# Stores of late projections issued from the ACT queue instead of the SP queue, in a one-core hybrid attention and S5 layer

## The chip, the cores and the metric

The kernel runs on one core of a Trainium2 chip. The metric is the time of one execution in microseconds of device time; for the kernel before, the median of three runs is 1052.14 us. The profile is of one execution whose own time is 1050.65 us and whose span from the first to the last instruction is 1048.8 us.

The engines are named as in the profile: PE (TensorE) multiplies matrices, DVE (VectorE), ACT (ScalarE) and POOL (GpSimd) work on elements, and SP (SyncE) does nothing but issue DMAs. ACT can issue DMAs too, between its other instructions. Each engine takes its instructions strictly in the order in which they stand in its queue, and an instruction that waits for a semaphore holds up everything behind it.

## The reference

One layer of a streaming encoder, for 1024 prompt tokens and 64 sample tokens (1088 columns in all), width 1024, in float32:

```python
h = rms_norm(x, g_norm) * (1.0 + scale[:, None, :]) + shift[:, None, :]
z = h @ w_in
zq, zk, zv, zqi, zki, zwi, zga, zu, zgs, zma, zmb = split_cols(z)
...
o_attn = dsa_attend(q, qi, wi, pos, k_all, v_all, ki_all, kpos, n_sel)
branch_a = (o_attn * jax.nn.silu(zga)) @ w_attn_proj
y_ssm, h_re, h_im = s5_mix(zu, h0, lambda_re, lambda_im, log_dt, ssm_b_re, ssm_b_im,
                           ssm_c_re, ssm_c_im, d_skip)
g_lin = jax.nn.gelu(y_ssm).astype(x.dtype) @ w_glu
y_glu = g_lin[..., :SSM_WIDTH] * jax.nn.sigmoid(g_lin[..., SSM_WIDTH:])
branch_b = (y_glu.astype(x.dtype) * jax.nn.silu(zgs)) @ w_ssm_proj
merged = jax.nn.sigmoid(zma) * branch_a + jax.nn.sigmoid(zmb) * branch_b
x = x + gate[:, None, :] * (merged @ w_out)
```

`dsa_attend` selects the best keys for each query by an indexer's scores and attends to them; `s5_mix` is a complex linear recurrence over the tokens.

## The kernel before, in words

Every product of float32 matrices is made of three products of parts: `hhi` and `hlo` are the normalized input, split into a high and a low part, `whi` and `wlo` the parts of a block of 128 columns of weights. L201 and L202 multiply `whi` with both parts of h, L206 `wlo` with the high one. A block of weights comes in two halves: for each, `load_split` has SP load `raw` (L163, 256 KB), ACT cast it to `whi` (L156) and POOL make the rest `wlo` (L157). The tiles `raw`, `whi` and `wlo` have two buffers each. The tokens are cut into three chunks of 384, 384 and 320 columns; a chunk of a block takes 8 matmuls of each of the three lines.

The projections q, u (zu), ma (zma), mb (zmb), the gate of attention (zga) and the gate of the S5 branch (zgs) are called late products here. One generator, `products(jobs)`, makes them block by block, and the program takes a few steps from it wherever another stage leaves PE free. So late products are woven into the index stage, the attention and the S5 stage, until about 800 us. Each chunk ends in an `evac`: ACT copies the result out of PSUM (`us` in `proj_u`, L604; `st` in `proj_store`, L611) or applies Silu (`sg` in `gate_s`, L627), and the chunk is stored to a tensor in HBM (`u_d`, L605; `q_d`, `ma_d` or `mb_d`, L612; `gs_d`, L628). These stores, 88 in all, are issued by SP.

The order within each engine's queue is the work of a scheduler, which orders what the program records by priorities and its own idea of times. `tc.issue_after(ins)` is a scheduling hint about what is recorded under it.

Around 720 to 770 us the S5 stage makes its outputs for blocks of groups, q = 0 to 3. SP loads the tables `tq` (L1342) and `cs` (L1347), then stores the outputs of the block before, eight stores `y_d<-yb` (L1447), stores `kp_d` (L1338), and loads the states `zq` (four loads of 136 KB, L1434). PE then computes with L1442 (`tq`) and L1443 (`zq` with `cs`), ACT copies the result to `yb` (L1444). Between them stand late products of `gate_s`. Later, four gelus on ACT (L1494, L1495), a split on DVE (L1496, L1497) and the GLU's products (L201, tiles `big`) follow.

In the built program each DMA that SP or ACT issues gets one of eight semaphores, DMAHW0 to DMAHW7, in turn; the order in which the scheduler records the DMAs of both queues decides whose turn it is. A DMA that takes a semaphore waits, in its engine's queue, until the DMA before it on that semaphore has landed.

Of the kernel before, what the change touches and what calls it, by code (L numbers as in the profile page):

```python
# [33 lines left out]
P = 128  # L34
# [23 lines left out]
BO = (7, 3, 4, 5, 6, 2, 1, 0, 8)  # L58
# [25 lines left out]
def hybrid_step(ctx, tc, ins, outs):  # L84
    nc = tc.nc
    act, dve, pool, pe, sync = nc.scalar, nc.vector, nc.gpsimd, nc.tensor, nc.sync
# [31 lines left out]
    def tmp(name="tmp"):  # L118
        return tmpp.tile([P, 384], F32, tag="tmp", name=name)

    q_d = dram.tile([4, P, TOK], F32, name="q_d")
    u_d = dram.tile([512, 8, NCH], F32, name="u_d")
# [3 lines left out]
    gs_d = dram.tile([4, P, TOK], F32, name="gs_d")  # L126
# [64 lines left out]
    last_mm = [None]  # L191
# [403 lines left out]
    stored = [None]  # L595

    def proj_u(m):
        def evac(c, t0, n, ps):
            s = tmp("us")
            npr = min(n, 1024 - t0)  # L600
            for o, w, n0 in ((0, npr, 8 + t0 // 8), (npr, n - npr, 0)):
                if w:
                    part = s[:, o:o + w].rearrange("p (s n) -> p s n", s=8)
                    act.copy(part, ps[:, o:o + w].rearrange("p (n s) -> p s n", s=8))  # L604
                    stored[0] = sync.dma_start(u_d[m * P:(m + 1) * P, :, n0:n0 + w // 8], part)  # L605
        return w_in, C_U + m * P, evac

    def proj_store(dst, c0, m):
        def evac(c, t0, n, ps):
            s = tmp("st")  # L610
            act.copy(s[:, :n], ps[:, :n])  # L611
            stored[0] = sync.dma_start(dst[m, :, t0:t0 + n], s[:, :n])  # L612
        return w_in, c0 + m * P, evac

    def gate_a(m):
# [7 lines left out]
    def gate_s(m):  # L623

        def evac(c, t0, n, ps):
            s = tmp("sg")
            act.activation(s[:, :n], ps[:, :n], AF.Silu)  # L627
            sync.dma_start(gs_d[m, :, t0:t0 + n], s[:, :n])  # L628
        return w_in, C_GS + m * P, evac

    jobs = [proj_store(q_d, C_Q, m) for m in range(4)] + [proj_u(m) for m in range(4)]
# [586 lines left out]
    ready = next(first)  # L1218
# [5 lines left out]
    def heads():  # L1224
        nonlocal ready
        pt = tokp.tile([P, 2, 2, 4, 2, P], F32R, tag="wtok", name="pt")
        keys, vals = kst, [vst]
        other = None
        for i, b in enumerate(BO):
            if b == 8:  # L1230
                ck = atq.tile([P, 4, P], F32, tag="qt", name="ck", bufs=1)
                sync.dma_start(ck, ins["cache_k"][0, 0].rearrange("(a p) g d -> p a (g d)", p=P))
                keys = rb.tile([P, 2, 2, 576], F32R, tag="t2", name="kss")
                build_keys(keys, None, [(ck[:, i], P) for i in range(4)] + [(ktok[:64, 8], 64)])
            st, mx = ready
            for h in range(8):
                other = Head(b, h, st, mx, keys, vals, pt, other)
                yield other
                if h == QH and b < 8:
                    ready = list(att_queries(BO[i + 1]))[1]  # L1240
                if h == VH and b == 8:
                    cv = atq.tile([P, 4, 2, 64], F32, tag="qt", name="cv", bufs=1)
                    sync.dma_start(cv, ins["cache_v"][0, 0].rearrange("(a p) g d -> p a g d", p=P))
                    vals.append(kvp.tile([P, 5, 2, 2, 64], F32R, tag="v", name="vss"))
                    split(vals[1][:, 0:4, :, 0, :], vals[1][:, 0:4, :, 1, :], cv)
                    split(vals[1][:64, 4, :, 0, :], vals[1][:64, 4, :, 1, :], vnew)
        for _ in range(3):
            yield None
# [179 lines left out]
    def ssm_out(q):  # L1428
        cs, tq = ca_t[q], tq_t[q]
        rs = slice(4 * q, 4 * q + 4)  # L1430
        zq = ssp.tile([P, 4, 2, NCH], F32, tag="eq", name="zq")
        for j in range(2):
            for g2 in range(2):
                sync.dma_start(zq[64 * j:64 * j + 64, :, g2, :], z4[64 * g2:64 * g2 + 64, j, rs, 0:NCH])  # L1434
        yield
        yb = ssp.tile([P, 8, NCH], F32, tag="yb", name="yb")
        for g0, ng in ((0, 3), (3, 3), (6, 2)):
            ps = bank1()
            for i in range(ng):
                g = g0 + i  # L1440
                o = ps[:, i * NCH:(i + 1) * NCH]
                pe.matmul(o, tq[:, g, :], uall[:, 8 * q + g, :], start=True, stop=False)  # L1442
                pe.matmul(o, cs[:, g // 2, g % 2, :], zq[:, g // 2, g % 2, :], start=False, stop=True)  # L1443
            act.copy(yb[:, g0:g0 + ng, :], ps[:, :ng * NCH].rearrange("p (g n) -> p g n", n=NCH))  # L1444
        yv = y_d[P * q:P * q + P].rearrange("(g c) t n -> c g t n", c=16)
        for t in range(8):
            sync.dma_start(yv[:, :, t, :], yb[16 * t:16 * t + 16])  # L1447
# [80 lines left out]
    for m in range(4):  # L1528
        w, nxt = nxt, load_pair(*pairs[m + 1])
        for t0, n in CH:  # L1530
            gs, s = two_tmps("gs", "sg")
# [34 lines left out]
    for m in range(8):  # L1566
        w = nxt
# [38 lines left out]
    for h in range(2):  # L1606
# [6 lines left out]
        for t in range(9):  # L1613
            t0, nt = tok_tile(t)
# [19 lines left out]
            dst = outs["y_prompt"][0, t0:t0 + nt] if t < NT else outs["y_sample"][0]  # L1634
# [61 lines left out]
```

## Time and profile before

| | |
|---|---|
| median of three runs (lowest, highest) | 1052.14 us (1051.26, 1052.95) |
| the profiled execution: own time, span | 1050.65 us, 1048.8 us |
| PE busy, share of the span | 978.5 us, 93% |
| DVE busy | 661.5 us, 63% |
| ACT busy | 459.0 us, 44% |
| POOL busy | 296.0 us, 28% |
| PE's longest waits | 11.56 us at 658.8 us, 9.52 us at 277.3 us, 5.05 us at 269.3 us |

The two waits near 270 and 277 us are for `whi` casts behind the selection of keys, the one at 658.8 us for an ACT instruction that stands behind a cast. In the attention, 300 to 545 us, PE is busy for 243.15 of 245 us. The granted clock of PE is full nearly everywhere and half for some microseconds after each of these long waits.

### The profile page before, as it was taken

What the parts mean: (1) busy time and instruction counts of PE and PEld (TensorE: products, weight loads), DVE (VectorE), ACT (ScalarE), POOL (GpSimd) and SP (SyncE); (2) the same over time, 40 slices, a digit from 0 to 9 for tenths busy, and PEclk for the clock granted to TensorE, in tenths of its full rate; (3) what the DMA queues carried; (4) which work ended last, traced back from release to release, by engine and by line L of the source; (5) the groups of instructions that cost most, each with busy time, mean ns of one, the idle gap of its engine ahead of it and who ended that gap; (6) DMA issues with size and microseconds to landing.
All of it is one profiled execution on the core that took longest, in us unless ns stands there. A gap on an engine that the chain in (4) does not pass through costs nothing.

```text
span 1048.8 us, 16634 instructions
## 1 busy us (share of the span) xinstructions
PE 978.5 (93%) x5948; PEld 887.9 (85%) x5948; DVE 661.5 (63%) x1400; ACT 459.0 (44%) x975; POOL 296.0 (28%) x438
## 2 busy tenths in 40 slices
PE   7777999999499999999998999599999999999997
PEld 1476887998389999999888999598999999998786
DVE  6774898899557777868647699900016556654244
ACT  3575567321167666666633321112273344442122
POOL 3475202531352211222117264454124000001200
PEclk9898999999699999999999999799999999999999
DMA  8730301153342211222248331344764354535133
GB/s 300 230 93 21 90 1 48 43 165 132 71 98 49 62 46 40 59 59 74 70 94 127 98 91 49 84 101 102 191 172 130 93 169 148 166 105 162 55 132 116
DMA packets 141765, 108.41 MB, mean 103 GB/s; under 512 B 32894, under 2 KB 128680, under 8 KB 141680
## 3 DMA queue, kind: packets, MB, share of 16 engines
q1 hardware_dynamic: 140160, 105.05, 36.1%
q10 hardware_dynamic: 1232, 2.23, 0.6%
q8 instruction: 47, 0.77, 0.3%
q14 instruction: 38, 0.31, 0.1%
q0 software_dynamic: 288, 0.05, 0.0%
HBM read 77.79 MB, written 25.17 MB: 98 GB/s over the span
## 4 chain that ended last, share of the span: by engine, by line
PE 61%; DVE 20%; ACT 5%; POOL 4%; issue 4%; DMA 3%; SPq 1%; POOLq 0%; DVEq 0%; ACTq 0%
PE acc L201 12%; PE acc L206 12%; PE acc L202 12%; PE o L1083 3%; PE big L201 3%; PE big L202 3%; PE big L206 3%; PE sc L1040 3%; PE tp L1066 3%; DVE gt L908 2%; DMA raw<-in_w_in 2%; DVE sc L706 2%; DVE near_v L915 1%; DVE t L1381 1%; POOL hlo L559 1%
## 5 line engine op out<-in xcount | busy, mean ns | idle before, releaser
L201 PE MATMUL acc<-hhi,whi 128*128 128x384 f32 (+1 forms) x768 | 257.2, 339 | 26.2 <-ACT whi L156 14.6
L202 PE MATMUL acc<-hlo,whi 128*128 128x384 f32 (+1 forms) x768 | 252.1, 333 | 0.0
L201 PEld LDWEIGHTS acc<-hhi,whi 128*128 128x128 f32 x768 | 146.5, 191 | 31.8 <-ACT whi L156 16.3
L157 POOL TENSOR_TENSOR wlo<-raw,whi 128x512 fp32r<-128x512 f32 x64 | 88.4, 1395 | 293.9 <-ACT whi L156 159.8
L206 PE MATMUL acc<-hhi,wlo 128*128 128x384 f32 (+1 forms) x768 | 150.1, 334 | 0.0
L202 PEld LDWEIGHTS acc<-hlo,whi 128*128 128x128 f32 x768 | 146.6, 191 | 0.6
L206 PEld LDWEIGHTS acc<-hhi,wlo 128*128 128x128 f32 x768 | 129.7, 190 | 1.9 <-POOL gw L1167 0.9
L156 ACT CAST whi<-raw 128x512 fp32r<-128x512 f32 x64 | 38.0, 620 | 72.3 <-DMA raw<-in_w_in 55.0
L1496 DVE CAST ghi<-gt 128x1088 fp32r<-128x1088 f32 x4 | 3.2, 808 | 103.1 <-DMA raw<-in_w_in 100.0
L1071 DVE TENSOR_TENSOR pt<-tp,pt 128x512 fp32r<-128x512 f32 (+3 forms) x112 | 57.0, 518 | 17.7 <-ACT pt L1070 16.8
L611 ACT COPY st<-acc 128x384 f32<-128x384 f32 (+1 forms) x60 | 27.9, 465 | 89.5 <-PE acc L206 86.7
L1050 ACT ACTIVATE pm<-pm,mx 128x1024 f32<-128x1024 f32 (+8 forms) x72 | 56.1, 779 | 24.7 <-DVE mx L1043 24.2
L1070 ACT CAST pt<-tp 128x512 fp32r<-128x512 f32 (+3 forms) x112 | 49.3, 450 | 35.9 <-PE tp L1066 34.6
L1631 POOL TENSOR_TENSOR yh<-yh,gfin 128x512 f32<-128x512 f32 (+1 forms) x9 | 11.6, 1292 | 173.3 <-ACT xr L1627 173.3
L1043 DVE CUSTOM_DVE_ANT_0 pm<-sc,bias 128x512 f32<-128x512 f32 (+4 forms) x72 | 42.6, 593 | 26.8 <-PE sc L1040 26.2
L201 PE MATMUL acc<-wohi,mhi 128*128 128x512 f32 (+2 forms) x152 | 56.7, 377 | 0.0
L202 PE MATMUL acc<-wolo,mhi 128*128 128x512 f32 (+2 forms) x152 | 56.7, 377 | 0.0
L1066 PE MATMUL tp<-ident,pm 128*128 128x128 f32 (+2 forms) x328 | 52.8, 270 | 0.7 <-DVE pt L1071 0.5
L1040 PE MATMUL sc<-kst,qs 128*128 128x512 f32 (+3 forms) x192 | 51.8, 352 | 0.1
L1083 PE MATMUL o<-pt,vst 128*128 128x256 f32 x288 | 47.6, 292 | 1.0 <-DVE pt L1071 0.9
L1066 PEld LDWEIGHTS tp<-ident,pm 128*128 128x128 f32 (+2 forms) x328 | 38.5, 139 | 9.7 <-DVE pt L1071 2.3
L706 DVE SCALAR_TENSOR_TENSOR sc<-relu,wi,sc 128x512 f32<-128x512 f32 (+5 forms) x42 | 42.8, 1020 | 3.8 <-ACT relu L704 1.0
(484 smaller groups left out, 2244.0 us busy)
## 6 DMA issues: line engine op xcount, KB each, us to landing
raw<-in_w_in SPq DMA_DIRECT2D x68, 256.0 KB
wm<-in_w_mod SPq DMA_DIRECT2D x16, 512.0 KB
xt<-in_x_prompt SPq DMA_DIRECT2D x8, 512.0 KB
gw<-in_w_mod SPq DMA_DIRECT2D x2, 2048.0 KB
raw<-in_w_out SPq DMA_DIRECT2D x16, 256.0 KB
xr<-in_x_prompt SPq DMA_DIRECT2D x16, 256.0 KB
ma_d<-st SPq DMA_DIRECT2D x16, 192.0 KB
mb_d<-st SPq DMA_DIRECT2D x16, 192.0 KB
```

The lines of the kernel that those rows point to most:

```text
L157: rest_on[0].tensor_tensor(lo, raw, hi.bitcast(F32), op=OP.subtract)
L201: pe.matmul(ps, lhi(k), rhi(k), start=(k == 0), stop=False)
L202: pe.matmul(ps, lhi(k), rlo(k), start=False, stop=False)
L206: last_mm[0] = pe.matmul(ps, llo(k), rhi(k), start=False, stop=(k == nk - 1))
L706: dve.scalar_tensor_tensor(scores[b][:nq], r[:nq, :n], w, scores[b][:nq], op0=OP.mult, op1=OP.add, accum_out=sums[:nq, 0, col] if h == 4 e ...
L1040: pe.matmul(ps, self.st[:, self.h // 2, self.h % 2, :nq], self.keys[:, self.h // 4, j, c:c + m], start=(j == 0), stop=(j == 1))
L1043: dve.tensor_tensor_reduce(out=self.pm[:, c:c + m], in0=ps, in1=bias[self.b][:nq, c:c + m], op0=OP.add, op1=OP.min, scale=-0.125, scalar=t ...
L1050: act.activation(self.pm, self.pm, AF.Exp, bias=self.ng, scale=-1.0, accum_out=self.sm)
L1066: pe.transpose(tp[:rows, i, :nq], self.pm[:, c0:c0 + rows], ident[:nq, :nq])
L1070: act.copy(d0, tp[:rows, i0:i1, :nq])
L1071: dve.tensor_tensor(d1, tp[:rows, i0:i1, :nq], d0.bitcast(F32), op=OP.subtract)
L1083: last_mm[0] = pe.matmul(o, v[:rows, kt, pr // 2].rearrange("p a d -> p (a d)"), pk[:rows, j, i, :, :nq], start=(kt == 0 and j == 0), stop ...
```

## The change

The three kinds of stores of late products, L605, L612 and L628, are issued by ACT instead of SP, right behind the ACT instruction that makes their data. Two groups of loads are recorded under `issue_after(last_mm[0].ins)`: the next block's queries in the attention (L1240 of the kernel before) and the S5 states `zq` (L1432 to L1434), whose two nested loops become one. Row by row, the program is the same with these two `issue_after` blocks and without them: the loads under them keep their place and their waits.

```diff
--- before.py
+++ after.py
@@ -602,14 +602,14 @@
                 if w:
                     part = s[:, o:o + w].rearrange("p (s n) -> p s n", s=8)
                     act.copy(part, ps[:, o:o + w].rearrange("p (n s) -> p s n", s=8))
-                    stored[0] = sync.dma_start(u_d[m * P:(m + 1) * P, :, n0:n0 + w // 8], part)
+                    stored[0] = act.dma_start(u_d[m * P:(m + 1) * P, :, n0:n0 + w // 8], part)
         return w_in, C_U + m * P, evac
 
     def proj_store(dst, c0, m):
         def evac(c, t0, n, ps):
             s = tmp("st")
             act.copy(s[:, :n], ps[:, :n])
-            stored[0] = sync.dma_start(dst[m, :, t0:t0 + n], s[:, :n])
+            stored[0] = act.dma_start(dst[m, :, t0:t0 + n], s[:, :n])
         return w_in, c0 + m * P, evac
 
     def gate_a(m):
@@ -625,7 +625,7 @@
         def evac(c, t0, n, ps):
             s = tmp("sg")
             act.activation(s[:, :n], ps[:, :n], AF.Silu)
-            sync.dma_start(gs_d[m, :, t0:t0 + n], s[:, :n])
+            act.dma_start(gs_d[m, :, t0:t0 + n], s[:, :n])
         return w_in, C_GS + m * P, evac
 
     jobs = [proj_store(q_d, C_Q, m) for m in range(4)] + [proj_u(m) for m in range(4)]
@@ -1237,7 +1237,8 @@
                 other = Head(b, h, st, mx, keys, vals, pt, other)
                 yield other
                 if h == QH and b < 8:
-                    ready = list(att_queries(BO[i + 1]))[1]
+                    with tc.issue_after(last_mm[0].ins):
+                        ready = list(att_queries(BO[i + 1]))[1]
                 if h == VH and b == 8:
                     cv = atq.tile([P, 4, 2, 64], F32, tag="qt", name="cv", bufs=1)
                     sync.dma_start(cv, ins["cache_v"][0, 0].rearrange("(a p) g d -> p a g d", p=P))
@@ -1429,8 +1430,8 @@
         cs, tq = ca_t[q], tq_t[q]
         rs = slice(4 * q, 4 * q + 4)
         zq = ssp.tile([P, 4, 2, NCH], F32, tag="eq", name="zq")
-        for j in range(2):
-            for g2 in range(2):
+        for j, g2 in ((0, 0), (0, 1), (1, 0), (1, 1)):
+            with tc.issue_after(last_mm[0].ins):
                 sync.dma_start(zq[64 * j:64 * j + 64, :, g2, :], z4[64 * g2:64 * g2 + 64, j, rs, 0:NCH])
         yield
         yb = ssp.tile([P, 8, NCH], F32, tag="yb", name="yb")
```

What moves is shown at two places. The first is SP's queue in the S5 stage, at the second block of outputs (`tq_8570`, `cs_8579`, `zq_8771`; `raw_8931` and `raw_9079` are weights of late products). Before, from the store of `kp_d` on:

```order
L1338 DMA kp_d_84<-kb_8751 32x4x128 [waits DMAHW1_49,Pool_49]
L1434 DMA zq_8771<-zs_7273 64x4x136 [waits DMAHW2_49,DVE_49]
L1434 DMA zq_8771<-zs_7273 64x4x136 [waits DMAHW3_49]
L1434 DMA zq_8771<-zs_7273 64x4x136 [waits DMAHW4_49]
L1434 DMA zq_8771<-zs_7273 64x4x136 [waits DMAHW5_49]
L628 DMA gs_d_83<-sg_8922 128x384 [waits DMAHW6_49,Activation_49]
L163 DMA raw_8931<-in_w_in 128x4x128 [waits DMAHW7_49]
L628 DMA gs_d_83<-sg_8965 128x384 [waits DMAHW0_49,Activation_49]
L628 DMA gs_d_83<-sg_9024 128x320 [waits DMAHW1_49,Activation_49]
L163 DMA raw_9079<-in_w_in 128x4x128 [waits DMAHW2_49]
L1532 DMA gssg_9623<-gs_d_83 128x320 [waits DMAHW3_49,DMAHW1_49]
```

The three stores of `gs_d` stand here behind the `zq` loads, each waiting for ACT. Now, from the second load of `cs` to the store of `kp_d` (after it come the four `zq` loads, then `raw_8931`, `raw_9079`):

```order
L1348 DMA cs_8579<-ca_8540 64x4x128 [waits DMAHW0_49]
L1348 DMA cs_8579<-ca_8540 64x4x128 [waits DMAHW2_49]
L1348 DMA cs_8579<-ca_8540 64x4x128 [waits DMAHW3_49]
L1448 DMA y_d_80<-yb_8627 16x8x136 [waits DMAHW4_49,Activation_49]
L1448 DMA y_d_80<-yb_8627 16x8x136 [waits DMAHW5_49]
L1448 DMA y_d_80<-yb_8627 16x8x136 [waits DMAHW6_49]
L1448 DMA y_d_80<-yb_8627 16x8x136 [waits DMAHW7_49]
L1448 DMA y_d_80<-yb_8627 16x8x136 [waits DMAHW0_49]
L1448 DMA y_d_80<-yb_8627 16x8x136 [waits DMAHW1_49]
L1448 DMA y_d_80<-yb_8627 16x8x136 [waits DMAHW2_49]
L1448 DMA y_d_80<-yb_8627 16x8x136 [waits DMAHW3_49]
L1339 DMA kp_d_84<-kb_8751 32x4x128 [waits DMAHW4_49,Pool_49]
```

On ACT, the same stretch reads now:

```order
L627 ACTIVATE sg_8922<-acc_8897 128x384 [waits PE_49,Activation_49]
L628 DMA gs_d_83<-sg_8922 128x384 [waits Activation_49]
L627 ACTIVATE sg_8965<-acc_8940 128x384 [waits PE_49]
L628 DMA gs_d_83<-sg_8965 128x384 [waits DMAHW5_49,Activation_49]
L627 ACTIVATE sg_9024<-acc_8999 128x320 [waits PE_49]
L628 DMA gs_d_83<-sg_9024 128x320 [waits DMAHW1_49,Activation_49]
L156 CAST whi_8925<-raw_8931 128x512 [waits DMAHW1_49]
L156 CAST whi_9077<-raw_9079 128x512 [waits DMAHW2_49,Pool_49]
L1445 COPY yb_8825<-tp_8826 128x408 [waits DMAHW5_49,DMAHW4_49,DMAHW6_49,DMAHW3_49,DMAHW7_49,DMAHW0_49,PE_49]
```

The stores have left SP's queue and stand behind their `sg`. In the turn of the semaphores the store of `sg_8922` has DMAHW2, that of `sg_8965` DMAHW5 and that of `sg_9024` DMAHW1. So the third row of SP now (`cs`, DMAHW2), the second `y_d` store after the first (DMAHW5) and the sixth `y_d` store (DMAHW1) wait until the store of `sg_8922`, `sg_8965` and `sg_9024` has landed.

The second place is the next block of outputs, with `zq_8935`. SP before (six of the twelve stores of `gs_d` stand in this stretch):

```order
L1434 DMA zq_8935<-zs_7273 64x4x136 [waits DMAHW1_49,DVE_49]
L1434 DMA zq_8935<-zs_7273 64x4x136 [waits DMAHW2_49]
L1434 DMA zq_8935<-zs_7273 64x4x136 [waits DMAHW3_49]
L1434 DMA zq_8935<-zs_7273 64x4x136 [waits DMAHW4_49]
L628 DMA gs_d_83<-sg_9074 128x384 [waits DMAHW5_49,Activation_49]
L628 DMA gs_d_83<-sg_9119 128x384 [waits DMAHW6_49,Activation_49]
L628 DMA gs_d_83<-sg_9154 128x320 [waits DMAHW7_49,Activation_49]
L628 DMA gs_d_83<-sg_9189 128x384 [waits DMAHW0_49,Activation_49]
L163 DMA raw_9194<-in_w_in 128x4x128 [waits DMAHW1_49,Pool_49]
L163 DMA raw_9198<-in_w_in 128x4x128 [waits DMAHW2_49,Pool_49]
L628 DMA gs_d_83<-sg_9227 128x384 [waits DMAHW3_49,Activation_49]
L628 DMA gs_d_83<-sg_9255 128x320 [waits DMAHW4_49,Activation_49]
```

SP now, the same `zq` loads and the weights behind them:

```order
L1435 DMA zq_8935<-zs_7273 64x4x136 [waits DMAHW0_49,DVE_49]
L1435 DMA zq_8935<-zs_7273 64x4x136 [waits DMAHW1_49]
L1435 DMA zq_8935<-zs_7273 64x4x136 [waits DMAHW2_49]
L1435 DMA zq_8935<-zs_7273 64x4x136 [waits DMAHW3_49]
L163 DMA raw_9198<-in_w_in 128x4x128 [waits DMAHW4_49,Pool_49]
L163 DMA raw_9288<-in_w_in 128x4x128 [waits DMAHW5_49,Pool_49]
L163 DMA raw_9292<-in_w_in 128x4x128 [waits DMAHW6_49,DMAHW4_49,Pool_49]
```

And ACT now:

```order
L627 ACTIVATE sg_9189<-acc_9164 128x384 [waits PE_49]
L628 DMA gs_d_83<-sg_9189 128x384 [waits DMAHW3_49,Activation_49]
L627 ACTIVATE sg_9227<-acc_9202 128x384 [waits DMAHW1_49,PE_49]
L628 DMA gs_d_83<-sg_9227 128x384 [waits DMAHW0_49,Activation_49]
L627 ACTIVATE sg_9255<-acc_9230 128x320 [waits PE_49]
L628 DMA gs_d_83<-sg_9255 128x320 [waits DMAHW3_49,Activation_49]
L156 CAST whi_9192<-raw_9198 128x512 [waits DMAHW4_49]
L156 CAST whi_9286<-raw_9288 128x512 [waits DMAHW5_49,Pool_49]
L1445 COPY yb_8968<-tp_8969 128x408 [waits DMAHW6_49,DMAHW2_49,DMAHW7_49,DMAHW1_49,PE_49]
```

The first `zq` load now takes DMAHW0 from the store of `sg_9227`, the last one DMAHW3 from the store of `sg_9255`, and `raw_9198` and `raw_9288` stand behind it; `raw_9194` now comes before the `tq` loads of this block. On PE, the first half of two chunks with `whi_9192` (16 matmuls) now comes before the products with `zq_8935`, where it came behind them.

## Rows read from the trace of the kernel before

**Rows 1.** Waits of PE over the whole span: total us, times, longest.

```profile
PE acc L201 <- ACT whi L156: 14.6, 2, 9.5
PE acc L201 <- ACT sg L619: 11.6, 1, 11.6
```

**Rows 2.** Three stretches: us, then busy of each engine, PE clock, DMA.

```profile
275.00:277.00 2.00, 2.00 (x8) 1.80 (x6) 1.96 (x2) 0.00 (x0) 0.77 (x1) 0.50 0.00 0
300.00:545.00 245.00, 243.15 (x1622) 224.61 (x1622) 182.35 (x466) 159.57 (x377) 53.38 (x45) 1.00 0.24 62
725.00:750.00 25.00, 24.50 (x159) 24.30 (x158) 0.00 (x0) 5.20 (x11) 3.88 (x3) 1.00 0.75 174
```

**Rows 3.** Waits of the SP queue, whole span: total us, times, longest.

```profile
SPq L612 <- ACT st L611: 154.3, 43, 10.3
...
SPq L1434 <- DVE zs L1426: 23.4, 1, 23.4
...
SPq L612 <- DMA uall<-u_d: 1.3, 2, 0.9
...
SPq L1532 <- DMA gs_d<-sg: 2.7, 1, 2.7
```

**Rows 4.** Timeline of the SP queue from 655 to 668 us.

```profile
661.03 1.26 SPq L1434 DMA_DIRECT2D zq<-zs  x2
...
665.02 0.99 SPq L163 DMA_DIRECT2D raw<-in_w_in  x2
```

**Rows 5.** Timeline of the SP queue from 715 to 766 us: start, duration.

```profile
725.11 3.88 SPq L1447 DMA_DIRECT2D y_d<-yb  x8
...
729.56 2.59 SPq L1434 DMA_DIRECT2D zq<-zs  x4
...
732.85 0.44 SPq L163 DMA_DIRECT2D raw<-in_w_in  x1
...
750.66 2.59 SPq L1434 DMA_DIRECT2D zq<-zs  x4
...
761.14 0.34 SPq L628 DMA_DIRECT2D gs_d<-sg  x1
```

**Rows 6.** Timeline of ACT from 715 to 805 us: start, duration, idle before.

```profile
728.30 0.49 ACT L627 ACTIVATE sg<-acc 128x384 f32<-128x384 f32 x1 [3.73 <-PE acc L206]
731.82 0.44 ACT L627 ACTIVATE sg<-acc 128x320 f32<-128x320 f32 x1 [3.03 <-PE acc L206]
736.74 0.62 ACT L156 CAST whi<-raw 128x512 fp32r<-128x512 f32 x1 [4.48 <-DMA raw<-in_w_in]
...
760.68 0.44 ACT L627 ACTIVATE sg<-acc 128x320 f32<-128x320 f32 x1 [3.02 <-PE acc L206]
...
777.35 1.28 ACT L1494 ACT_TABLE_LOAD   x1 [0.40 <-DMA yt<-y_d]
778.64 2.22 ACT L1494 ACTIVATE gt<-yt 128x1024 f32<-128x1024 f32 x1
```

**Rows 7.** Timeline of PE, around 735 to 739 and 760 to 764 us.

```profile
734.84 0.39 PE L1443 MATMUL tp<-zq,cs 128*128 128x136 f32 x2
...
738.75 0.42 PE L201 MATMUL acc<-hhi,whi 128*128 128x384 f32 x1
...
760.43 0.39 PE L1443 MATMUL tp<-zq,cs 128*128 128x136 f32 x2
...
763.70 0.42 PE L201 MATMUL acc<-hhi,whi 128*128 128x384 f32 x1
```

**Rows 8.** DMA activity from 760.5 to 764 us in 40 slices, tenths busy.

```profile
DMA  0000000000000000079998400000000000000000
```

**Rows 9.** Stores that ACT issues near the end: ns least, median, most.

```profile
L1637 ACTq DMA_DIRECT2D out_y_prompt<-yh x8: 359/360/408, 1001.9 to 1040.0; - x8
```

**Rows 10.** Timeline of DVE from 775 to 800 us.

```profile
790.74 0.73 DVE L1496 CAST ghi<-gt 128x1088 fp32r<-128x1088 f32 x1 [1.04 <-ACT gt L1495]
791.50 1.29 DVE L1497 TENSOR_TENSOR glo<-gt,ghi 128x1088 fp32r<-128x1088 f32 x1
```

## The prediction

> **What bounds the kernel now.** I read the waits of PE first. PE is the bound: in the attention it works 243.15 of 245 us [rows 2], and over the whole span it has only three long waits, two for casts of weights (14.6 us together) and one of 11.6 us for ACT, where late products run into weights that SP has not loaded yet [rows 1]. So a change to stores can gain only where a load that PE waits for comes earlier, and loses wherever a load comes after PE's need of it. Hence the second view, the waits of the SP queue: SP stands 154.3 us behind stores L612 whose copies ACT has not made [rows 3]. That looks like a large reserve, but while SP stands there PE is not waiting. The third view is the timelines of SP, ACT and PE between 715 and 770 us, because there the order shows SP's loads taking the semaphores of stores that ACT issues late. In this stretch PE still works 24.50 of 25 us while the DMA engines are 0.75 busy [rows 2]: nothing is lost there before, and nothing is spare.
>
> That a DMA without any need of another's data waits for it, by its semaphore, is seen before: the stores L612 waited 1.3 us for landings of `uall` loads, which have nothing to do with them [rows 3].
>
> **The stores leave SP.** Durations are those of the profiled execution, so the sum starts from its own 1050.65 us; it is 1.5 us below the median of 1052.14. ACT takes 0.36 us to issue a store [rows 9]; 88 of them are 31.7 us over some 630 us. ACT is busy 159.57 of 245 us in the attention [rows 2], so its idle time covers them; if each third of those in the attention came between PE and its next data, it would be about 4 us. I take +0.5, bounds 0 and +4.
>
> Where SP gains: the `zq` loads at 661.03 wait for DVE (23.4 us in the waits of SP [rows 3]), and weights stand behind them. PE's 11.6 us end with these weights. Four `zq` loads at 0.65 us end at 663.65, but with two stores among them and behind them the weights go out at 665.02 [rows 4, 5]. The stores gone, that is 1.3 us: **-1.3** (bounds -1.4 and 0). The order of `zq` and weights, and so the rest of this wait, stays. The first two long waits hang on DVE's selection and on ACT; no row of the order moves weights ahead there: 0.
>
> The two `issue_after` blocks move no row: 0. The loads of `uall` at about 545 us now wait for two stores by their semaphores, but other loads of the same tensor still go after them: 0, at most one landing, 3.2 us (below).
>
> **How long a store takes to land.** It decides everything that follows. A store alone is issued at 761.14 [rows 5]; the last bytes move in the 24th of 40 slices from 760.5 to 764 us, so at 762.6 [rows 8]: 1.5 us, the lower bound. In a full stretch SP waited 2.7 us for a landing of `gs_d` [rows 3], after issuing one more load of about 0.5 us: 3.2 us. The stores here go out among `cs` and `y_d` transfers, in between: I take 2.4, for a `zq` load too, whose last one is issued until 732.15 and is no wait for PE at 734.84 [rows 5, 7]. A load of weights takes longer: issued at 732.85, cast at 736.74, 3.9 us [rows 5, 6].
>
> **First stop, 735 us.** Silu `sg_9024` ends at 732.26 [rows 6]; its store, now right behind it on ACT, lands at 734.7. The sixth `y_d` store of SP has its semaphore. Before, it went out at 725.11 + 5 x 0.485 = 727.5 [rows 5]; now it waits until 734.7. Queued behind it on SP: two `y_d` stores and `kp_d` (until 736.6), the four `zq` loads (until 739.2), `raw_8931` at 739.2 and `raw_9079` at 739.65. PE wants `zq` at 734.84 [rows 7] and gets its third load at 737.9 + 2.4 = 740.3: 5.5 us idle. Then the weights are late next: 743.1 and 743.6, two casts at 0.62 until 744.2. The copy of `yb` stands behind both casts on ACT, 744.7, and PE's last eight products of this block wait for it: 0.9 us, or 1.8 at half clock. Late products go on at 745.6 to 746.5 instead of 738.75 [rows 7]: 6.9 to 7.8 us. After a wait of 5.05 us PE's granted clock was 0.50, its lower level, 1.2 of 2.4 GHz [rows 1, 2], so half clock is likely here: **+7.4** (6.0 with the short landing, 8.7 with the long one).
>
> **Second stop, 760 us before, 768 after.** All of PE is 7.4 later. `sg_9255` ends at 761.12 + 7.4 = 768.5 [rows 6], its store lands at 770.9, and the last `zq` load waits for it (before: 750.66 + 3 x 0.65 = 752.6 [rows 5]). Behind it `raw_9198` goes out at 771.55 and `raw_9288` at 772.0. PE would want `zq` at 760.43 + 7.4 = 767.8 [rows 7], but 16 matmuls now come first. A chunk of 320 columns takes 731.82 - 728.30 = 3.52 us [rows 6], one of 384 so 4.22, and a matmul of its 24 takes 0.176: 2.8 us, to 770.6. `zq` is there at 773.3, the weights at 775.5 and 775.9, both cast by 776.7, `yb` copied by 777.2, the last eight products done at 778.1. Less the 2.8 us of work already done, that is 775.3 against 763.70 + 7.4 = 771.1 [rows 7]: **+4.2** (3.3 and 5.9).
>
> **The gelus.** They now stand on ACT behind the copy of the third following chunk, since `yt` is loaded late too. From the end of that chunk: copy 0.48 (as the Silus), store 0.36, table 1.28, four gelus at about 2.2, in between two copies, a cast and a store (1.94 together) [rows 6, 9], then on DVE 0.73 and 1.29 for the split [rows 10]: 14.9 us. PE has three chunks meanwhile (4.22 + 4.22 + 3.52) and seven matmuls of the GLU, 13.2 us: **+1.7** (0 and 4).
>
> **The sum.** 0.5 - 1.3 + 7.4 + 4.2 + 1.7 = +12.5, so 1050.65 + 12.5 = 1063. The low ends give 8 (1058.6), all high ends together 26, which I don't expect together: 1058 to 1072 for this case.
>
> **Rivals.** *No change:* the stores land before SP comes to the rows that wait, because something else holds SP as long, or the weights are hidden anyway; then only -1.3 and +0.5 are left, 1049.9. Against it: SP came to the sixth `y_d` store 7.2 us before that landing, to the last `zq` load 10.9 us before (752.6 against 761.12 + 2.4), and PE had no slack [rows 2].
>
> *Faster:* SP no longer stands behind copies, and weights overtake what they stood behind. The place is the wait of 11.6 us [rows 1]. If the weights came before the `zq` loads, it would go altogether, 1039; if only the two stores go and the attention gives back its 1.85 us of idle time, 1047.5. It decides if no store's semaphore is met late, that is if a store landed within a few tenths of its Silu's end, against the 1.5 us of the lone store [rows 5, 8]. The Trainium skill speaks for this rival: "Perfetto Trace Analysis", section "DMA Optimizations", says that giving inputs to one DMA-issuing engine and outputs to another may allow more dynamic spread. By it the time would be the 1039 to 1047.5 of this rival; no row here shows such a split, and the wait rows of SP agree only that stores hold its loads up.
>
> *Larger:* landings of 3.2 us in the full stretch at both stops, the gelus at 4, and ACT's issues on the path in the attention: 1072 to 1080.
>
> **Chances.** Forecast 0.72, larger 0.10, no change 0.08, faster 0.10. What a measurement here can tell from no change is about 0.2%, 2.1 us; so slower 0.82, same 0.08, faster 0.10. The range leaves out the faster case and the upper part of the larger one: 1052 to 1073.
>
> **What would show it.** SP's timeline has a gap before one of the last `y_d` stores near 728 to 735 us, ended by the landing of a `gs_d` store, and another before the last `zq` load near 770. PE has a wait of 5 to 6 us at 735 for `zq`, then half clock, and a shorter one at 771 to 776. The wait at 658.8 us is about 10.3 instead of 11.6. The attention is as long as before. It is wrong if PE does not wait at 735 us (then the semaphores are met in time, or the store lands much sooner), if the attention grows (then ACT's issues are on the path), or if the waits are there and PE does other work in them.

## The result, and the profile after

The changed kernel takes 1064.51 us (median of 4 runs, 1062.96 to 1067.34), the kernel before in the same comparison 1052.55 us (4 runs): a ratio of 1.0128, 95% interval 1.0107 to 1.0149. It is 12 us slower; 1063 was forecast. The profiled execution took 1063.17 us, its span 1061.3 us.

To see where the time goes, I matched the matmuls of the two traces one by one, in order, and took how much later each starts than in the kernel before ("pace", in us; minus is ahead). The columns are places in the kernel before; rows 1 to 12 are the experiments below. Each row is one traced execution, and executions of one kernel differ (that of run 6 took 1062.39 us, its median is 1058.83).

| kernel | 649 us | 678 | 710 | 728 | 744 | 776 | 793 | 809 | 1039 |
|---|---|---|---|---|---|---|---|---|---|
| changed | -3.2 | -5.4 | -5.1 | -6.7 | -0.1 | +4.2 | +4.2 | +12.4 | +12.4 |
| 1 | -0.6 | -2.7 | -2.5 | -4.1 | -2.7 | -2.7 | -2.2 | -2.2 | -2.2 |
| 2 | +0.5 | 0.0 | 0.0 | -1.7 | +5.9 | +9.8 | +9.8 | +18.7 | +18.7 |
| 3 | +1.9 | -0.2 | 0.0 | -1.6 | 0.0 | 0.0 | 0.0 | +8.0 | +8.0 |
| 4 | -1.6 | -3.1 | -3.1 | -4.7 | +2.4 | +6.3 | +6.3 | +11.7 | +11.7 |
| 5 | -1.9 | -3.5 | -3.5 | -5.1 | -1.9 | -1.9 | -1.9 | +11.4 | +11.9 |
| 6 | +0.8 | -12.1 | -1.7 | -6.3 | -5.6 | -5.6 | -4.6 | +11.4 | +11.8 |
| 7 | +4.7 | -8.2 | +1.8 | -2.8 | -2.2 | -2.7 | -2.7 | +9.5 | +10.4 |
| 8 | -1.9 | -2.8 | -2.8 | -2.8 | +4.0 | +8.4 | +16.7 | +16.7 | +16.7 |
| 9 | 0.0 | -0.5 | -0.5 | -0.6 | -0.2 | -0.2 | +7.2 | +7.2 | +7.1 |
| 10 | +0.7 | -12.2 | -2.4 | -6.9 | -6.4 | -6.3 | +6.9 | +6.9 | +7.4 |
| 11 | -1.0 | -13.9 | -13.6 | -11.0 | -11.6 | -4.9 | -0.3 | -0.3 | +0.9 |
| 12 | -1.4 | -14.3 | -13.4 | -10.8 | -11.4 | -5.0 | +0.8 | +0.8 | +0.9 |

So the changed kernel loses in three places only: +6.7 us between 728 and 744, +4.3 between 744 and 776, +8.2 between 793 and 809. Before them it was ahead by 6.7 us, after them nothing changes any more. The stretches of the profile after show the same (us, busy of PE, PEld, DVE, ACT, POOL, PE clock, DMA):

```profile
300.00:545.00 245.00, 242.52 (x1614) 224.28 (x1615) 183.65 (x466) 158.46 (x375) 50.61 (x43) 1.00 0.24 61
725.00:750.00 25.00, 19.40 (x117) 19.10 (x116) 0.00 (x0) 5.53 (x11) 5.12 (x4) 0.86 0.67 164
760.00:800.00 40.00, 36.44 (x224) 35.77 (x223) 3.50 (x5) 18.89 (x28) 6.42 (x5) 1.00 0.55 155
800.00:850.00 50.00, 44.46 (x255) 43.76 (x254) 31.90 (x40) 19.08 (x33) 12.34 (x4) 0.93 0.30 94
```

In the attention PE is busy for 0.6 us less than before [rows 2]; 725 to 750 us has lost 5.1 us of PE's work and some of its clock. From 760 to 800 and from 800 to 850 us PE was never idle before; now 3.6 and 5.5 us are. Before, these two stretches read:

```profile
760.00:800.00 40.00, 40.00 (x252) 39.99 (x251) 9.66 (x11) 25.18 (x37) 8.81 (x7) 1.00 0.59 171
800.00:850.00 50.00, 50.00 (x302) 50.00 (x301) 32.23 (x46) 18.56 (x38) 11.20 (x4) 1.00 0.33 99
```

PE's waits, as in [rows 1]:

```profile
PE acc L201 <- ACT whi L156: 12.9, 2, 7.8
PE acc L201 <- ACT sg L619: 10.4, 1, 10.4
...
PE tp L1444 <- DMA zq<-zs: 6.6, 2, 5.6
...
PE big L202 <- DVE glo L1498: 3.0, 1, 3.0
PE big L201 <- DVE ghi L1497: 2.5, 1, 2.5
```

The two waits for `whi` near 270 us are 1.7 us shorter together, the wait for the weights at 660 us is 1.2 us shorter. The wait for `zq` and the two of the GLU are new. What SP waits for between 715 and 800 us:

```profile
SPq L1435 <- DMA gs_d<-sg: 7.5, 2, 5.0
SPq L1448 <- DMA gs_d<-sg: 6.2, 3, 2.5
SPq L1479 <- DMA gs_d<-sg: 5.3, 2, 3.2
SPq L1493 <- DMA ma_d<-st: 3.4, 1, 3.4
...
SPq L1348 <- DMA gs_d<-sg: 2.8, 2, 2.3
```

Loads of `zq`, `yt` and `cs` and stores of `y_d` and of the final states (L1479) have no need of `gs_d` or `ma_d`. They wait for landings of those stores because the store holds the semaphore whose turn it is: 25.2 us of SP in all. SP's timeline shows what that delays (compare [rows 5]):

```profile
722.08 7.29 SPq L1448 DMA_DIRECT2D y_d<-yb  x8
...
729.96 2.60 SPq L1435 DMA_DIRECT2D zq<-zs  x4
732.60 1.22 SPq L163 DMA_DIRECT2D raw<-in_w_in  x2
...
759.58 5.08 SPq L1435 DMA_DIRECT2D zq<-zs  x4
764.76 6.75 SPq L163 DMA_DIRECT2D raw<-in_w_in  x4
...
788.24 0.82 SPq L1493 DMA_DIRECT2D yt<-y_d  x2
```

The eight `y_d` stores took 3.88 us before and take 7.29. The second four `zq` loads took 2.59 and take 5.08. The `yt` loads go out at 788.24, before at 773.55 (SP's timeline before):

```profile
773.55 0.81 SPq L1492 DMA_DIRECT2D yt<-y_d  x2
```

ACT's side of the first stop and of the third (as [rows 6]):

```profile
725.14 0.44 ACT L627 ACTIVATE sg<-acc 128x320 f32<-128x320 f32 x1 [3.03 <-PE acc L206]
725.61 0.35 ACTq L628 DMA_DIRECT2D gs_d<-sg  x1
735.81 0.62 ACT L156 CAST whi<-raw 128x512 fp32r<-128x512 f32 x1 [10.23 <-DMA raw<-in_w_in]
...
792.24 0.43 ACT L611 COPY st<-acc 128x320 f32<-128x320 f32 x1 [0.51 <-PE acc L206]
...
793.21 1.28 ACT L1495 ACT_TABLE_LOAD   x1 [0.54 <-DMA yt<-y_d]
```

The cast of the weights stands 10.23 us behind a load. The gelus' table load is at 793.21 instead of 777.35 and stands behind the third copy `st`. On PE (timeline, as [rows 7]):

```profile
733.98 0.79 PE L1444 MATMUL tp<-zq,cs 128*128 128x136 f32 x2 [5.60 <-DMA zq<-zs]
...
738.80 0.43 PE L201 MATMUL acc<-hhi,whi 128*128 128x384 f32 x1
...
807.86 0.44 PE L201 MATMUL big<-ghi,whip 128*128 128x384 f32 x1 [2.49 <-DVE ghi L1497]
811.35 0.69 PE L202 MATMUL big<-glo,whip 128*128 128x384 f32 x1 [3.04 <-DVE glo L1498]
...
813.11 0.52 PE L201 MATMUL big<-ghi,whip 128*128 128x384 f32 x1
...
816.42 0.34 PE L201 MATMUL big<-ghi,whip 128*128 128x384 f32 x1
```

On DVE there, timeline (the durations of [rows 10] in its first row, not in the others):

```profile
803.58 1.29 DVE L1498 TENSOR_TENSOR glo<-gt,ghi 128x1088 fp32r<-128x1088 f32 x1
805.77 2.04 DVE L1497 CAST ghi<-gt 128x1088 fp32r<-128x1088 f32 x1 [0.90 <-ACT gt L1496]
807.84 3.45 DVE L1498 TENSOR_TENSOR glo<-gt,ghi 128x1088 fp32r<-128x1088 f32 x1
811.22 5.92 DVE L157 TENSOR_TENSOR wlop<-raw,whip 128x512 fp32r<-128x512 f32 x2
```

And on POOL, timeline:

```profile
804.25 12.34 POOL L1544 TENSOR_TENSOR olo<-oT,ohi 128x1088 fp32r<-128x1088 f32 x4 [12.66 <-PE acc L206]
```

The same cast takes 2.04 us instead of 0.73 and the same subtraction 3.45 instead of 1.29 as soon as POOL makes `olo`.

### The profile page after: what moved, and what is told of

Same layout as the page of the kernel before. It is cut to its first block, busy times and chain, and to the rows that moved or that the text cites. A ratio compares the mean times of both kernels' runs of the same rounds, so it can differ in the third digit from the quotient of the medians.

```text
span 1061.3 us, 16501 instructions
## 1 busy us (share of the span) xinstructions
PE 982.1 (93%) x5948; PEld 891.3 (84%) x5948; DVE 662.7 (62%) x1400; ACT 459.8 (43%) x975; POOL 296.9 (28%) x438
## 4 chain that ended last, share of the span: by engine, by line
PE 63%; DVE 15%; DMA 6%; ACT 6%; POOL 5%; issue 4%; SPq 1%; ACTq 0%; POOLq 0%; DVEq 0%
PE acc L206 12%; PE acc L201 12%; PE acc L202 11%; PE o L1083 3%; PE big L206 3%; PE big L202 3%; PE big L201 3%; PE tp L1066 3%; PE sc L1040 3%; DMA raw<-in_w_in 2%; DVE t L1382 2%; PE tp L202 1%; PE tp L201 1%; PE tp L206 1%; DVE sc L706 1%
## 5 line engine op out<-in xcount | busy, mean ns | idle before, releaser
L201 PE MATMUL acc<-hhi,whi 128*128 128x384 f32 (+1 forms) x768 | 257.5, 340 | 23.2 <-ACT whi L156 12.9
L157 DVE TENSOR_TENSOR wlop<-raw,whip 128x512 fp32r<-128x512 f32 x24 | 21.0, 878 | 112.6 <-PE acc L206 112.5
L1632 POOL TENSOR_TENSOR yh<-yh,gfin 128x512 f32<-128x512 f32 (+1 forms) x9 | 11.6, 1290 | 180.5 <-ACT xr L1628 180.5
```

Of the source, the lines that this page charges most:

```text
L157: rest_on[0].tensor_tensor(lo, raw, hi.bitcast(F32), op=OP.subtract)
L201: pe.matmul(ps, lhi(k), rhi(k), start=(k == 0), stop=False)
```

## The experiments

My theory: the three stops come from `gs_d` (and in the third also `ma_d`) stores that take semaphores out of SP's turn, so that SP's loads wait for landings. The main rival: ACT's own issues, or the moved stores as such, cost the time. Ratios are to the kernel before, on the same chip, with their 95% interval.

**1. The gate's stores back on SP.** Of the change, the stores of `u`, `q`, `ma` and `mb` stay on ACT:

```diff
-            act.dma_start(gs_d[m, :, t0:t0 + n], s[:, :n])
+            sync.dma_start(gs_d[m, :, t0:t0 + n], s[:, :n])
```

> The changed kernel with the gs_d stores alone (L628, 12 of the 88) back on SP; the other 76 stay on ACT. Theory (turn of the semaphores): no store of ACT is met late any more after 720 us, so the three stops of the changed kernel at 728, 761 and 805 us (6.7, 4.3 and 8.2 us of PE's pace) go away, and the lead of 6.75 us that PE had by 721 us stays: 1064.5 - 19.2 = 1045.3, between 1044 and 1048, faster than the kernel before. Rival (the load on ACT or the moved queue as a whole costs the time): only a share of the 12 us comes back, 12 stores of 88, so 1062 to 1064.

Measured: 1048.24 us (10 runs), 0.9971 [0.9961, 0.9981]. The three stops are gone (1.4 us stay between 728 and 744, with waits of 1.1 us for `yb` and 0.2 us besides), and the kernel is now faster than before by 2.7 us. This is the fastest version of the study. It gained less than expected, because it was ahead by 4.1 us at 728 us where the changed kernel was by 6.7, and lost 1.9 of that later (on the lead, see below). The gelus begin as early as before, with copies behind them (ACT's timeline):

```profile
774.72 1.28 ACT L1495 ACT_TABLE_LOAD   x1 [0.47 <-DMA yt<-y_d]
```

**2. The gate's stores alone on ACT.** The kernel before, with the opposite edit of one line:

```diff
-            sync.dma_start(gs_d[m, :, t0:t0 + n], s[:, :n])
+            act.dma_start(gs_d[m, :, t0:t0 + n], s[:, :n])
```

> The kernel before with the gs_d stores alone issued by ACT. Theory: the three stops are there in full and the early lead is not: 1052.5 + 6.7 + 4.3 + 8.2 = 1071.7, between 1068 and 1074, slower than the changed kernel. Rival (load of 88 stores on ACT): 12 of 88 stores cost next to nothing, 1052 to 1055.

Measured: 1071.58 us, 1.02 [1.0155, 1.0245], with all three stops (7.6, 4.0 and 8.9 us by pace). One of the three lines of the change makes the whole loss: the 12 `gs_d` stores do it, all in the S5 stage, not the 88 as such. This kernel has neither of the two `issue_after` blocks, so the stops do not need them.

**3. The gate's stores on POOL.** In this program POOL's DMAs have semaphores of their own, so SP and ACT no longer share one with these stores:

```diff
-            act.dma_start(gs_d[m, :, t0:t0 + n], s[:, :n])
+            pool.dma_start(gs_d[m, :, t0:t0 + n], s[:, :n])
```

> The changed kernel with the gs_d stores issued by POOL, whose DMAs have semaphores of their own; they stay off SP's queue as in the change. Theory: SP's cs, y_d and zq rows then take semaphores of SP's own earlier loads, so the stops at 728 and 761 us vanish as with the stores back on SP, 1045 to 1049. Rival (the stops come from the stores having left SP's queue, by another order of SP's rows or DMA traffic in the stretch): the stops stay, 1060 to 1065. If issuing on POOL is slow, up to 2 us more.

Measured: 1058.10 us, 1.0062 [1.0038, 1.0087]. The stops at 735 and 765 us are gone (of the first, 1.6 us stay, with waits of 0.7 us for `yb` and 0.8 us besides), with the same stores off SP as in the change; so it is not their leaving SP that makes them. This run takes them off ACT too. That ACT's work for them is not the cause either is seen in the changed kernel, where ACT issues such a store in 0.35 us and then stands idle for 10.23 us behind SP's load. What is left is the shared semaphore. But the third stop stays in full (8.1), which I had not expected. SP's waits:

```profile
SPq L1493 <- DMA ma_d<-st: 4.6, 1, 4.6
```

ACT's timeline:

```profile
788.83 1.28 ACT L1495 ACT_TABLE_LOAD   x1 [0.54 <-ACT st L611]
```

`yt` still waits for an `ma_d` store's semaphore, and the gelus stand behind the third copy.

**4. `olo` on DVE.** Of the changed kernel, with the order of PE, ACT and SP as it was:

```diff
-        pool.tensor_tensor(olo[:, m], oT[:, m], ohi[:, m].bitcast(F32), op=OP.subtract)
+        dve.tensor_tensor(olo[:, m], oT[:, m], ohi[:, m].bitcast(F32), op=OP.subtract)
```

> The changed kernel with the four subtractions olo (L1544) on DVE behind its GLU splits instead of on POOL; orders of PE, ACT and SP are the same. In the changed kernel the last cast and split before the GLU took 2.04 and 3.45 us on DVE while POOL ran olo, 0.73 and 1.29 us otherwise. Theory (contention of POOL's olo with DVE makes most of the GLU stop): the stop falls from 8.2 us to 2 to 3, so 1058 to 1060. Rival (the gelus are late anyway): 1063 to 1065. The first two stops stay in either case.

Measured: 1063.43 us, 1.0121 [1.0096, 1.0146]. DVE's durations are back:

```profile
808.84 0.73 DVE L1497 CAST ghi<-gt 128x1088 fp32r<-128x1088 f32 x1 [1.63 <-ACT gt L1496]
809.61 1.29 DVE L1498 TENSOR_TENSOR glo<-gt,ghi 128x1088 fp32r<-128x1088 f32 x1
```

PE's waits there fall from 5.5 to 2.8 us, the stop from 8.2 to 5.3. So some 2.8 us of the third stop are DVE beside POOL; the rest is late gelus, more than I had expected to be left: the time is the rival's.

**5. The gate's and the late `ma` and `mb` stores on POOL.** The `gs_d` stores and the six late ones of `ma` and `mb`, so that `yt` meets no store's semaphore:

```diff
-            act.dma_start(gs_d[m, :, t0:t0 + n], s[:, :n])
+            pool.dma_start(gs_d[m, :, t0:t0 + n], s[:, :n])
...
-    gates_ab = [proj_store(dst, c0, m) for m in range(8) for dst, c0 in ((ma_d, C_MA), (mb_d, C_MB))]
+    gates_ab = [proj_store(dst, c0, m, pool if 2 * m + i >= N_ATT else act)
+                for m in range(8) for i, (dst, c0) in enumerate(((ma_d, C_MA), (mb_d, C_MB)))]
```

> As the run with the gs_d stores on POOL, and the last two ma_d and mb_d blocks' stores (6 stores of L612, recorded after the gate of S5) on POOL too, so that the load of yt takes no semaphore of a store of ACT. On ACT the gelus still stand behind the third copy st, as in the changed kernel. Theory (the order on ACT, with POOL's olo beside it, makes the GLU stop): the stop of 8 us stays, 1057 to 1060. Rival (yt waits for the landing of a ma_d store, and that makes the GLU stop): the stop goes, 1048 to 1051.

Measured: 1063.65 us, 1.0101 [1.0074, 1.0128]. This is slower than either forecast. SP loads `yt` 2.8 us later than before and 12 us earlier than in the change, yet ACT stands at the copies. SP's timeline:

```profile
776.30 2.27 SPq L1494 DMA_DIRECT2D yt<-y_d  x2
```

ACT's timeline:

```profile
786.25 0.43 ACT L611 COPY st<-acc 128x320 f32<-128x320 f32 x1 [0.55 <-PE acc L206]
786.70 1.28 ACT L1496 ACT_TABLE_LOAD   x1
```

With the gelus behind the third copy an early `yt` does not take the stop away; it is even 13.3 us. But most of that is DVE beside POOL again. DVE's timeline, and POOL's:

```profile
801.51 8.60 DVE L1499 TENSOR_TENSOR glo<-gt,ghi 128x1088 fp32r<-128x1088 f32 x1
801.62 7.34 POOL L1545 TENSOR_TENSOR olo<-oT,ohi 128x1088 fp32r<-128x1088 f32 x3
```

The last `glo` takes 8.60 us instead of 1.29, the cast before it 2.06 instead of 0.73. PE waits 10.2 us for the two; without these 8.6 us of excess some 1.6 us of the waits would be left (an estimate from these rows). So this run does not price the order on ACT by itself.

**6 and 7. The weights before `zq`.** The largest wait in this region is the one for weights at 660 us, which stand behind the first block's `zq` loads on SP. In run 6 (experiment 1's kernel) and run 7 (the kernel before) these loads are recorded two steps later and behind the last weight load (the first edit of the diff is for the `zq` loads of all four blocks, the second for the first block alone):

```diff
-            with tc.issue_after(last_mm[0].ins):
+            with tc.issue_after(last_raw[0].ins):
                 sync.dma_start(zq[64 * j:64 * j + 64, :, g2, :], ...)
...
+            if q == 0:
+                for _ in range(2):
+                    yield
```

> The version with the gs_d stores on SP, and the four zq loads of the first block recorded two steps later and held behind the last load of weights on SP's own queue (issue_after on that load instead of on a matmul). In SP's queue the next two loads of weights now stand before the zq loads that wait for DVE, where they stood behind. Theory (PE's wait of 10.3 us near 656 us is the weights standing behind zq): the wait falls to 0 to 3 us and the half clock behind it goes too, 1048.2 - 10 = 1038, between 1035 and 1043. Rival (PE runs into another wait at once, since zq and the DVE scan end no earlier): 1046 to 1049.

> The kernel before, all stores on SP, with only the same change of the zq loads of the first block (two steps later, behind the last load of weights). If the weights before zq are what counts, 1052 - 10 = 1042, between 1038 and 1046: the stores on ACT are worth 3 us beside it, no more. If the stores on SP hold the weights back again, 1048 to 1052.

Measured: 1058.83 us, 1.0056 [1.0036, 1.0077], and 1058.5 us, 1.0049 [1.0032, 1.0067]. Both are slower than any forecast of theirs. In both, the wait is gone and PE is 12.9 us further at 678 us than it was at 649, as the rival "faster" had it; but 10 us go back before 710, since two weight loads, which go out only at 686.70 in run 6, then stand ahead of `tq` and `cs` on SP, and PE waits for `cs` (run 6):

```profile
PE tp L1445 <- DMA cs<-ca: 6.5, 1, 6.5
```

Then the GLU stops for 16.0 and 12.2 us. The first `yt` loads go out at 786.50 and 783.04 us, and in run 6 the gelus wait for them, not for a copy (ACT's timeline):

```profile
790.49 1.28 ACT L1500 ACT_TABLE_LOAD   x1 [3.86 <-DMA yt<-y_d]
```

The last `glo` again runs beside `olo` in both, 3.56 and 3.48 us. What each of the two costs here was not tried apart.

**8. The copies behind the gelus.** The changed kernel; the copies `st` of the last products are put behind the gelus on ACT, PE's order unchanged:

```diff
-            act.copy(s[:, :n], ps[:, :n])
+            with tc.issue_after(gelus[AFTER_GELU[min(n_late[0], 5)]].ins):
+                act.copy(s[:, :n], ps[:, :n])
```

> The changed kernel with the copies of the late products' sums recorded behind the gelus on ACT: the first two behind the first 1,024-column gelu pair of blocks 0 and 1, the next behind the later ones. TensorE's order, SP's order (but for one pair of weight loads) and every store's engine stay as changed. Theory A (the gelus come late because ACT stands in them behind copies that wait for products): the first two stops stay at +6.7 and +4.3 us, the third falls from 8.2 us to 0 to 3, and the time is 1056 to 1060 us. Rival B (the gelus come late because their loads do, whatever stands ahead of them on ACT): the third stop stays within 2 us of 8.2 and the time at 1062 to 1066. Rival C: the copies, now late, leave TensorE without a free accumulator, and a wait for ACT's copies takes the place of the third stop; 1062 or more.

Measured: 1068.35 us, 1.0159 [1.0139, 1.0178]. PE no longer waits for `ghi` or `glo`, but it loses 8.3 us in another row of its waits:

```profile
PE acc L201 <- ACT st L614: 6.4, 1, 6.4
```

ACT's timeline:

```profile
793.50 1.28 ACT L1501 ACT_TABLE_LOAD   x1 [2.10 <-DMA yt<-y_d]
```

Theory A of this run fell, B and C hold together: nothing stood ahead of the gelus, yet they began at 793.50, at the landing of `yt`; and the copies behind them gave PE no accumulator.

**9. As 8, with the gate's stores on POOL.** The edits of 3 and 8 together.

> The changed kernel with the gs_d stores issued by POOL (which took away the first two stops, 1058.10 us, third stop 8.1) and the late products' copies recorded behind the gelus on ACT. Theory A (two separate causes that add): no stop is left but 0 to 3 us of the third, 1050 to 1053 us. Rival B (the gelus come late whatever stands ahead of them on ACT): 1057 to 1059. Rival C (TensorE waits for the late copies): 1057 or more.

Measured: 1056.88 us, 1.0038 [1.0023, 1.0053]: just under the rivals' 1057. The first two stops are gone; `yt` goes out at 778.03, 4.5 us later than before, the table load is at 782.90, 5.6 later, and PE waits 4.3 us for `st` and loses 7.3 us.

**10. As 6, with the edit of 8.**

> The kernel of the weights-first run (gs_d stores on SP, the first block's zq loads behind the last raw load; 1058.83 us, 4.6 us ahead of before until the third stop, then 16 us lost there) with the late products' copies recorded behind the gelus on ACT. Theory A: the stop of 16 us falls to 0 to 5 and the time is 1045 to 1052 us. Rival B (gelus late whatever stands ahead of them): 1057 to 1061.

Measured: 1057.0 us, 1.0039 [1.002, 1.0057], the rival's time. PE, 6.3 us ahead, waits 11.4 us for `st`.

**11 and 12. The weights before `zq` without the wait for `cs`.** As 6 for the first block alone, with two weight loads behind the next block's `cs` loads; 12 has the edit of 8 too:

```diff
-        last_raw[0] = sync.dma_start(raw, src)
+        n_raw[0] += 1
+        if last_cs[0] is not None and 4 < n_raw[0] <= 6:
+            with tc.issue_after(last_cs[0].ins):
+                last_raw[0] = sync.dma_start(raw, src)
+        else:
+            last_raw[0] = sync.dma_start(raw, src)
```

> The first undo run (gs_d stores on SP, 1048.24 us) with the zq loads of the first block alone put behind the weights that TensorE waits for, and with two of the weight loads after them put behind the next block's cs loads, which stood behind them in the weights-first run and cost TensorE a wait of 6.5 us there. Theory: the wait of 10.3 us goes (12 us ahead of before after it, as in the weights-first run), 0 to 3 us come back between 690 and 715, and the time is 1038 to 1045 us. Rival: the S5 blocks' own chain on POOL and DVE does not come earlier with TensorE, so the gelus, here again behind two copies, stop the GLU for what was gained: 1048 to 1058.

> The kernel of the run before with the late products' copies recorded behind the gelus, in the order on ACT that the first undo run has. Theory: as there, 1038 to 1045 us, with no wait of TensorE for ghi or glo. Rival (the gelus' loads come late against a TensorE that is ahead): TensorE waits for the copies instead, for ACT's st, and the time is 1048 to 1058. Where the two runs differ by under 2 us, the order of copies and gelus is no cost by itself.

Measured: 1051.4 us, 0.9991 [0.9979, 1.0004], and 1052.34 us, 1.0005 [0.9992, 1.0018], the rivals' times. The gain of 13 us is kept until 710 us and then given back piece by piece, to POOL's tables, to `zq` and `yb` and to a cast (waits of PE of run 11 from 680 us):

```profile
PE tp L1338 <- POOL ca L1329: 3.4, 1, 3.4
PE acc L208 <- ACT whi L156: 2.8, 1, 2.8
PE tp L1453 <- ACT yb L1455: 2.8, 2, 2.2
PE tp L1454 <- DMA zq<-zs: 2.3, 2, 2.2
```

Up to 776 us that is S5's chain of tables, loads and outputs: of a lead of 13.6 us at 710, 5.0 are left. The cast stands on ACT behind two of the gelus. Their `yt` loads go out at 772.49 us in run 11, only 1.1 us earlier than before, though the last stores of the states go out 6.2 us earlier (763.91 for 770.14): on SP three `gs_d` stores stand between, the last of which goes out at 771.52, behind its Silu. So the 10.3 us wait of PE hid other chains that end nearly as late; taking the wait away gives PE nothing. The two runs differ by 0.9 us, so no cost of the order of copies and gelus by itself is seen here.

## Why the prediction was right

**First stop: right in mechanism and size** (+7.4 forecast, +6.7 measured). The sixth `y_d` store waits for the landing of the last chunk's store, `zq` and the weights stand behind it, PE waits 5.60 us for `zq` (5.5 forecast) and runs at half clock after it. The two `y_d` waits and the loads' start fit the landing of 2.4 us that I took between 1.5 and 3.2. Runs 2 and 3 show the cause: the loss comes with the twelve `gs_d` stores alone, and goes, but for 1.6 us, when the same stores have other semaphores.

**Second stop: right** (+4.2 forecast, +4.3 measured), with the waits on the `zq` load that the prediction named.

**Stores gone from SP: right in size at its place.** The weights go out 4.8 us earlier by the clock, of which 3.5 is the whole stretch being earlier (`zq` at 657.53 instead of 661.03): 1.3 us, as forecast. PE's wait is 1.2 us shorter here, and 10.2 to 10.6 us in every run that leaves the order of `zq` and weights and has these stores on ACT, against 11.1 in run 2, which has not. The pace gains 2.2 us between 649 and 678 us here, in others of these runs 0.5 to 2.2.

**ACT issues: +0.5 forecast, and no more is seen.** Between 300 and 545 us the pace loses 0.7 us here, 0.7 to 0.8 in runs 1, 3, 4, 5, 8 and 9, which have these issues too, and 0.2 in run 2, which has not. Run 1 keeps 76 of the 88 issues and is faster than before.

**The lead was not foreseen, and is not fully settled.** The forecast left the changed kernel 0.8 us ahead when it comes to the first stop; by pace it was 6.7. Its pieces:

- Near 270 us a step of the prediction failed: it put the change of the two waits for casts at 0. They are 12.9 us here for 14.6 [rows 1], 12.6 to 13.3 in all ten runs with the stores of `u`, `q` and most of `ma` and `mb` on ACT, and 15.0 and 14.9 in runs 2 and 7, which keep them on SP. Between 250 and 300 us the pace gains 2.4 us here, 0.9 to 2.5 in runs 1, 3, 4, 5, 8 and 9, and nothing in run 2. Which row of the order gives that was not tried.
- The weights at 660 us are 2.2 us of it.
- A further 1.6 us come between 710 and 728, where the granted clock was 0.93 in the trace before (700 to 725 us) and 1.00 after. As far as the traces show, that is luck: PE waits 1.8 us for POOL's `ca` there in the kernel before, the changed one and runs 1, 3, 5, 8 and 9 alike, and from 715 to 720 us the clock was then 0.66, 0.74 and 0.66 in the traces of the kernel before and of runs 8 and 9, which don't have the 1.6 us, and 1.00 in the others.
- At 649 us the lead is 3.2 us already, where runs 1, 3, 4 and 8, with the same stores on the same engines up to there, were ahead by 0.6, behind by 1.9, and ahead by 1.6 and 1.9. So executions differ by some 5 us in that part, and how much of the 3.2 us belongs to the change stays open.

**The gelus: the step that was mis-sized**, +1.7 forecast (0 to 4), +8.2 measured. The place was right: the gelus stand behind the third copy and PE runs out of chunks; counted from that copy, at 792.24, the 13.2 us of work that the prediction gave PE end at 805.4, and PE's wait begins there. What was missing: the split on DVE at 0.73 and 1.29 us, taken from rows without POOL beside it, takes 2.04 and 3.45 (run 4: 2.8 us of the stop); and after 5.5 us of waits PE runs at half clock until 816.42, so the loss is 2.7 us more than the waits. I had put half clock into the first stop and not into this one. The error of 6.5 us here and the unforeseen lead of 5.9 us cancelled by luck, and so the total was close for a partly wrong reason.

**What makes the third stop** is three things that were not all priced apart. `yt` is loaded late: in runs 8 and 9 nothing stands ahead of the gelus, yet they start when `yt` lands, 16.2 and 5.6 us later than before, and PE then lacks the accumulators whose copies stand behind them. The gelus stand behind the third copy: in run 5 `yt` is early and the stop stays. And the last split then runs beside POOL's `olo`: 2.8 us of the stop in run 4, and in run 5 8.6 us of its 10.2 us of waits. The kernel before and run 1, whose gelus start at 777.35 and 774.72, are without the stop. That semaphores are all that can delay `yt` is not so: in run 9 it went out 4.5 us late without meeting a store's semaphore. What delayed it there was not tried apart.

**The rival "faster"** is partly true, and only for some stores. Moving the stores of `u`, `q`, `ma` and `mb` gained (run 1, 0.9971), moving those of `gs` lost (run 2, 1.02). The Trainium skill ("Perfetto Trace Analysis", section "DMA Optimizations") says that one engine for inputs and another for outputs may make sense. Run 1 agrees with that and run 2 does not; no run here splits inputs and outputs wholly, as SP keeps the stores of `y_d` and others.

## What to carry to other kernels

Before moving a DMA to another queue, read which semaphores it shares and with whom. Where queues take semaphores in turn, a store that is issued late by one engine holds up the loads of another that have nothing to do with it; what counts is how late its data is made, not how long its issue takes. The price of an instruction holds for the neighbours that its row had: moved beside POOL's `olo`, a split of 2.0 us took 5.5. And a long wait in a profile is worth only as much as the next chain behind it leaves: here 10.3 us of waiting, once removed, gave nothing at the end.

## What the runs showed of the hardware that was not expected

DVE and POOL slow each other. A DVE cast of 128x1088 took 2.04 us beside POOL's `olo` against 0.73 without, the subtraction 3.45 against 1.29, a subtraction of 128x512 2.96 (5.92 for two) against 0.69. With `olo` on DVE the cast and the subtractions were back at 0.73, 1.29 and 0.68 us, and the four `olo` took 4.89 us there against 12.34 on POOL. In the changed kernel's trace the four `olo` end at 807.22, 810.15, 813.66 and 816.60 us, and each DVE instruction that starts beside one ends 0.5 to 1.2 us after it, about its own time: the cast at 807.81, the subtraction at 811.29, the two of 128x512 at 814.21 and 817.14. POOL pays too: an `olo` takes 2.5 us where no DVE instruction ends within it (run 5), 3.0 to 3.6 us here.

The Trainium skill says why ("SBUF — State Buffer", section "Who interferes with whom"): a DVE instruction with two inputs in SBUF and a GpSimd instruction that reads SBUF contend for a shared port. A DVE cast can do so too, in a two-port mode, and whichever of the two was issued first then blocks the other for the whole of its instruction. The rows above agree, and so does the kernel before, where beside `olo` the product `sg<-big,sg`, with `big` in PSUM, took 0.56 us and `sg<-sg,gs` 2.22, against 0.56 away from it. That this cast is in such a mode is not shown. Run 5 goes further: there `glo` started at 801.51 us by the records, 0.1 us before the second `olo`, and ended 1.15 us after the fourth, so it was let in between none of them. POOL's start times in a trace are rough, and what decides whether a waiting DVE instruction gets in between two of POOL's was not tried. The effect was there to be read in the kernel before, too, where the two `wlop` beside `olo` took 6.02 us (DVE's timeline before):

```profile
799.95 6.02 DVE L157 TENSOR_TENSOR wlop<-raw,whip 128x512 fp32r<-128x512 f32 x2 [5.95 <-ACT whip L156]
```
